# MLP up stage of a decoder trunk: four Winograd products added up in one PSUM bank with reads in between, and the P1 and P2 of three units in front

## The chip, the core and the metric

The kernel runs on one core of one Trainium2 chip. The metric is the device time of one execution in microseconds (us). The time before is 1290.3 us, the median of 3 runs (1288.57 to 1290.55). One more execution was recorded by the hardware profiler; it took 1287.94 us, and all rows of a profile below come from it.

## The reference

One layer of a decoder trunk on 1024 tokens with 1024 features: an attention sub-layer of three head groups, a gated MLP, a gated embedding, a final norm. The change is in the up half of the MLP. Cut to it:

```python
def _conv_ffn(h, w_gate, w_up, conv_w, conv_b, w_down):
    gate = h @ w_gate                       # (1024, 1024) x (1024, 2816)
    gate = causal depthwise conv of width 3 along the tokens, + conv_b
    return (jax.nn.gelu(gate) * (h @ w_up)) @ w_down
...
    h2 = _rmsnorm(r, ffn_norm[i])
    r = r + _conv_ffn(h2, w_gate[i], w_up[i], conv_w[i], conv_b[i], w_down[i])
```

All is f32. A product of two f32 matrices is made of three fp32r matmuls (`mm3`: high part of the weights by high and low part of the data, low part of the weights by the high part of the data; lines 117, 118, 119).

## The kernel before

**The units.** The 2816 columns of `w_gate` and `w_up` are taken 128 at a time: 22 units `f`. A unit makes `gs` (128 gate columns x 1024 tokens) and `us` (128 up columns x 1024 tokens), convolves `gs` into `cv`, takes its gelu, multiplies `us` by it and sends `us` to device memory (`h3_dram[f]`, line 987), from where the next stage, down, reads it.

**Seven products.** Gate and up rows, the two halves of the 1024 features and the two halves of the tokens (left, right: 512 each) make a 2 x 2 x 2 block product, and it is done with seven products in Winograd's form instead of eight. `prod(n)` is product Pn: 4 slices of 128 features by 3 matmuls, 12 matmuls of 128 x 512. With `g0` and `g1` the left and right half of `gs`, `u0` and `u1` those of `us`:

```
g0 = P1 + P2
g1 = P1 + P6 + P5 + P3
u1 = P1 + P6 + P5 + P7
u0 = P1 + P6 + P7 + P4
```

`B[n][k]` are the data operands: 1 and 2 are halves of the normalised data, 5, 3, 6, 7, 4 are made of sums and differences (`minus`, then `form`, which splits into high and low with one ScalarE cast and one VectorE subtraction, `hl`, lines 772 and 773). They are made once, after the norm `rs2`. `A[n]` are the weight operands: 1 and 2 are the halves of the gate weights (`weights_up_1`, tiles `whi`, `wlo`, two buffers each, printed `whig` and `wlog`), the rest come of sums of gate and up weights (`weights_up_2`, tiles `s13`, `s24`, `f13`, `f24`, `f4`). The loads `wg` (gate) and `wu` (up) are issued on SP's queue; `wg` lands in the one buffer `wraw`, `wu` in one of four buffers `ws`.

**PSUM before.** Bank `a` (`pg`, 3 buffers) takes P1, which ScalarE copies to `s1`, and then P2 is added to it there: `g0`. Bank `d` (`b1`, 5 buffers) takes P5 and then P3, bank `b` (`b1`) P6, P7 and P4. `s1` is added to what is read of banks `b` and `d` by VectorE: in `plus(g1, "b", s1)`, in `after5`, and in `plus(u0, "b", s1)`.

**Order.** The program is written unit after unit; a scheduler of the language places each instruction on its engine's queue by priority and by its own estimate of readiness, and it ran ahead: matmuls of unit f+1 and f+2 stand among those of f. Each engine then runs its queue strictly in order. `tc.high_priority(offset=n)` moves what is in it earlier. `gs`, `us` and `cv` have one buffer each, so that unit f+1's `gs` is written after unit f's convolution has read its own.

**The start.** Units 0 and 1 run P1 and P2 first (`early`), since `B[1]` and `B[2]` are ready before the other five operands are formed; then follow the rests. For unit 1, `s1` lies in another tile (`s1x`).

Of the kernel before, what the change touches and what calls it, by code (L numbers as in the profile page):

```python
# [17 lines left out]
F32 = mybir.dt.float32  # L18
# [4 lines left out]
ALU = mybir.AluOpType  # L23
# [52 lines left out]
def trunk(ctx: ExitStack, tc: tile.TileContext, a, out, dbg):  # L76
# [830 lines left out]
    class Unit:  # L907


        def __init__(self, f, A, s1=None):  # L910
            self.f, self.A = f, A
            self.bank = {"a": pg(f"ga{f}")}
            self.s1 = fp.tile([P, H2], F32, tag="s1", bufs=1, name=f"s1{f}") if s1 is None else s1

        def prod(self, n, to, first=False):
            if to not in self.bank:
                self.bank[to] = b1(f"g{to}{self.f}")
            wh, wl = [x.rearrange("p (k c) -> p k c", k=4) for x in self.A[n]]
            for k in range(4):
                xh, xl = B[n][k]  # L920
                mm3(self.bank[to], wh[:, k, :], wl[:, k, :], xh, xl, first and k == 0, k == 3, not first)

        def early(self):

            self.prod(1, "a", True)
            S.copy(self.s1, self.bank["a"])
            self.prod(2, "a")

        def rest(self):
            f, bank, s1 = self.f, self.bank, self.s1  # L930
# [7 lines left out]
            def plus(out, to, x):  # L938
                V.tensor_tensor(out=out, in0=bank[to], in1=x, op=ALU.add)  # L939

            def g0_done():
                S.copy(g0, bank["a"])

            def after5():
                S.copy(u1, bank["d"])  # L945
                V.tensor_tensor(out=u1, in0=u1, in1=s1, op=ALU.add)  # L946

            def g1_done():
                plus(g1, "d", g1)
                S.activation(cv, gs, AF.Identity, bias=col(C_CB + f), scale=w(2))  # L950
                V.scalar_tensor_tensor(out=cv[:, 1:], in0=gs[:, :T - 1], scalar=w(1), in1=cv[:, 1:],
                                       op0=ALU.mult, op1=ALU.add)
                V.scalar_tensor_tensor(out=cv[:, 2:], in0=gs[:, :T - 2], scalar=w(0), in1=cv[:, 2:],  # L953
                                       op0=ALU.mult, op1=ALU.add)
                S.activation(cv, cv, AF.Gelu_apprx_tanh)  # L955

            if f == 0:
                g0_done()
                self.prod(5, "d", True)
                after5()  # L960
                self.prod(3, "d")
                self.prod(6, "b", True)
                plus(g1, "b", s1)
                g1_done()
                self.prod(7, "b")
                plus(u1, "b", u1)
            else:
                if f == 1:
                    g0_done()
# [3 lines left out]
                self.prod(6, "b", True)  # L973
                plus(g1, "b", s1)
                self.prod(5, "d", True)
                after5()
                if f > 1:
                    self.prod(2, "a")
                    g0_done()
                self.prod(7, "b")  # L980
                plus(u1, "b", u1)
                self.prod(3, "d")
                g1_done()
            self.prod(4, "b")
            plus(u0, "b", s1)
            V.tensor_tensor(out=us, in0=us, in1=cv, op=ALU.mult)  # L986
            G.dma_start(h3_dram[f], us)  # L987

    lft = [t[:, half(0)] for t in r]
# [7 lines left out]
        form(5, j, lft[j], "big")  # L997
    with tc.high_priority(offset=3000):
        raw, A1 = weights_up_1(1)
    for j in range(4):  # L1000
        norm(j + 4, 1, rs2)
        form(3, j, rgt[j + 4], "big")
# [7 lines left out]
        minus(lft[j + 4], lft[j + 4], lft[j])  # L1010
        form(4, j, lft[j + 4], "r")

    s1x = cp.tile([P, T], F32, tag="rs", bufs=1, name="s1x")
# [290 lines left out]
```

## Time and profile before

| | |
|---|---|
| runs | 1290.55, 1288.57, 1290.3 us |
| profiled execution | 1287.94 us, span of its instructions 1286.2 us |
| mean granted TensorE clock | 0.994 |
| TensorE (PE) | busy 1261.6 us, 98% of the span |
| VectorE (DVE), ScalarE (ACT), GpSimd (POOL) | busy 840.8, 536.8, 103.6 us |
| MLP up stage | from 508.06 us (first matmul into `ga`) to 934.73 us (first matmul of down) |

A row of the timeline has the start in us from the start of the span, the duration in us, engine, source line, operation, output<-inputs, shape, count, and in brackets the idle time of the engine before it with what ended it. Matmuls are pipelined: one of them takes 0.39 us from start to modelled end, but the next starts long before that, so the distance of starts is what counts. A row of a window has its bounds and length, and for each engine the busy time and, behind an x, the instructions that started in it, then the granted clock of PE, the share of the DMA engines and GB/s.

### The profile page before, as it was taken

The numbers are of one execution on the slowest core, as the hardware profiler recorded it, in microseconds if no ns is written. First come the engines' busy times: TensorE is split into PE (matmuls) and PEld (weight loads), VectorE is DVE, ScalarE is ACT, GpSimd is POOL, SyncE is SP. The second block draws the span as 40 slices with busy tenths as digits, with TensorE's granted clock in tenths as the row PEclk, the third lists the DMA queues.
The fourth block names the chain that finished last, engine by engine and source line by source line (L and its number), as shares of the span: only waits on it lengthen the run. The fifth ranks groups of instructions, "written<-read, shape, count | busy, mean of one in ns | idle before, by whom it ended". The sixth has DMA issues, their size and how long they took to land.

```text
span 1286.2 us, 16285 instructions
## 1 busy us (share of the span) xinstructions
PE 1261.6 (98%) x6330; PEld 1059.1 (82%) x6330; DVE 840.8 (65%) x1410; ACT 536.8 (42%) x842; POOL 103.6 (8%) x113
## 2 busy tenths in 40 slices
PE   9999999999999999999999999999999999999996
PEld 7888888887888887788788888888888888888896
DVE  7986967567776478967776676677456123346576
ACT  6324143257675256544444334334235123334432
POOL 2000000013111231000000000000000021001010
PEclk9999999999999999999999999999999999999998
DMA  7110110111004735232222122223457216323132
GB/s 250 50 34 17 34 33 19 48 33 34 18 17 153 281 131 188 66 98 82 82 83 98 67 81 98 76 88 96 160 165 251 75 54 202 105 90 115 42 107 82
DMA packets 42237, 122.30 MB, mean 95 GB/s; under 512 B 5168, under 2 KB 7728, under 8 KB 42160
## 3 DMA queue, kind: packets, MB, share of 16 engines
q1 hardware_dynamic: 32032, 89.14, 21.4%
q0 software_dynamic: 8544, 30.41, 6.4%
q10 hardware_dynamic: 1584, 1.71, 0.4%
q8 instruction: 49, 0.80, 0.3%
q14 instruction: 28, 0.23, 0.1%
HBM read 97.13 MB, written 24.12 MB: 94 GB/s over the span
## 4 chain that ended last, share of the span: by engine, by line
PE 68%; issue 11%; POOL 2%; DVE 2%; ACT 1%; DMA 0%; DVEq 0%; POOLq 0%; ACTq 0%
PE d L119 6%; PE d L118 6%; PE d L117 6%; PE gb L119 3%; PE gb L117 3%; PE gb L118 3%; PE gd L117 2%; PE pg L117 2%; PE gd L119 2%; PE pg L119 2%; PE pg L118 2%; PE gd L118 2%; PE ga L119 2%; PE ga L118 2%; PE ga L117 2%
## 5 line engine op out<-in xcount | busy, mean ns | idle before, releaser
L119 PE MATMUL ga<-b,wlog 128*128 128x512 f32 x176 | 68.6, 390 | 0.5 <-DVE wlog L773 0.5
L117 PE MATMUL ga<-b,whig 128*128 128x512 f32 x176 | 68.9, 392 | 0.1
L117 PE MATMUL gb<-b,f 128*128 128x512 f32 x176 | 68.8, 391 | 0.0
L118 PE MATMUL gb<-b,f 128*128 128x512 f32 x176 | 68.7, 391 | 0.0
L118 PE MATMUL ga<-b,whig 128*128 128x512 f32 x176 | 68.6, 390 | 0.0
L119 PE MATMUL gb<-b,f 128*128 128x512 f32 x176 | 68.6, 390 | 0.0
L117 PE MATMUL pg<-hp,hpg 128*128 128x256 f32 (+1 forms) x192 | 61.7, 321 | 0.0
L773 DVE TENSOR_TENSOR l<-h3r,h 128x1024 fp32r<-128x1024 f32 x32 | 38.9, 1224 | 33.8 <-ACT h L772 33.6
L119 PE MATMUL pg<-hp,lpg 128*128 128x256 f32 (+1 forms) x192 | 61.0, 318 | 0.0
L118 PE MATMUL pg<-lp,hpg 128*128 128x256 f32 (+1 forms) x192 | 61.0, 318 | 0.0
L772 ACT CAST h<-h3r 128x1024 fp32r<-128x1024 f32 x34 | 35.5, 1051 | 39.9 <-PE d L118 19.2
L955 ACT ACTIVATE cv<-cv 128x1024 f32<-128x1024 f32 x22 | 23.4, 1062 | 68.2 <-DVE cv L953 68.2
L946 DVE TENSOR_TENSOR us<-us,s 128x512 f32<-128x512 f32 x21 | 14.5, 691 | 52.0 <-ACT us L945 52.0
L987 POOL DMA_DIRECT2D h3d<-us x22 | 11.7, 534 | 418.3 <-DVE us L986 418.3
L781 POOL TENSOR_TENSOR acc<-acc,sq 128x512 f32<-128x512 f32 (+1 forms) x15 | 29.1, 1938 | 166.1 <-ACT sq L780 165.8
L117 PEld LDWEIGHTS ga<-b,whig 128*128 128x128 f32 x176 | 33.0, 188 | 8.6 <-ACT s L972 1.4
L945 ACT COPY us<-gd 128x512 f32<-128x512 f32 x22 | 12.9, 588 | 64.9 <-DMA h3d<-us 59.8
L119 PEld LDWEIGHTS ga<-b,wlog 128*128 128x128 f32 x176 | 33.0, 188 | 7.9 <-DVE wlog L773 1.0
L117 PEld LDWEIGHTS gb<-b,f 128*128 128x128 f32 x176 | 33.3, 189 | 7.1 <-DVE gs L939 0.2
L119 PEld LDWEIGHTS gb<-b,f 128*128 128x128 f32 x176 | 33.2, 188 | 6.9
L118 PEld LDWEIGHTS gb<-b,f 128*128 128x128 f32 x176 | 33.2, 189 | 6.9
L118 PEld LDWEIGHTS pg<-lp,hpg 128*128 128x128 f32 x192 | 36.6, 191 | 2.6 <-DVE lp L1081 0.2
(778 smaller groups left out, 3864.2 us busy)
## 6 DMA issues: line engine op xcount, KB each, us to landing
wu<-w_gu SPq DMA_DIRECT2D x22, 512.0 KB, 3.6
wg<-w_gu SPq DMA_DIRECT2D x22, 512.0 KB, 3.5
h3d<-us POOLq DMA_DIRECT2D x22, 512.0 KB, 2.9
h3r<-h3d SPq DMA_DIRECT2D x22, 512.0 KB, 3.6
wr_wo<-w_out SPq DMA_DIRECT2D x16, 512.0 KB, 3.7
h3r<-h3d POOLq DMA_DIRECT2D x12, 512.0 KB, 3.9
x<-xT SPq DMA_DIRECT2D x16, 256.0 KB, 5.5
r<-xT SPq DMA_DIRECT2D x16, 256.0 KB, 6.8
```

What stands on the lines that cost most here:

```text
L117: TE.matmul(o, wh, xh, start=first, stop=False, skip_group_check=on)
L118: TE.matmul(o, wh, xl, start=False, stop=False, skip_group_check=on)
L119: TE.matmul(o, wl, xh, start=False, stop=last, skip_group_check=on)
L772: S.copy(hi, src)
L773: e.tensor_tensor(out=lo, in0=src, in1=hi.bitcast(F32), op=ALU.subtract)
L781: e.tensor_tensor(out=acc[:, cols], in0=acc[:, cols], in1=sq[:, cols], op=ALU.add)
L945: S.copy(u1, bank["d"])
L946: V.tensor_tensor(out=u1, in0=u1, in1=s1, op=ALU.add)
L955: S.activation(cv, cv, AF.Gelu_apprx_tanh)
L987: G.dma_start(h3_dram[f], us)
```

## The change

Product P1 goes into bank `b` as the first of a group, and P6, P7 and P4 are added to it there, in this order. The bank is read in between: after P1 (ScalarE copies it to `g0`), after P6 (ScalarE copies P1 + P6 to `g1`), after P7 (VectorE adds it to `u1`) and after P4 (VectorE multiplies it by the gelu's left half, straight into `u0`). P2 has bank `a` alone and VectorE adds it to `g0`; P5 and P3 share bank `d` as before. `s1` and `s1x` are gone. The last product of 1024 columns becomes two of 512, one of them reading the bank.

At the start P1 and P2 of units 0, 1 and 2 run before the rest. The gate weights of unit 2 are therefore loaded early, into a buffer of `ws` instead of `wraw`, and the second half of its weight work stands after unit 1's rest with a raised priority.

```diff
     def weights_up_1(f):
-        g = f4("wraw", f"wg{f}")
+        g = f4("ws" if f == 2 else "wraw", f"wg{f}")
...
-        def prod(self, n, to, first=False):
-            if to not in self.bank:
-                self.bank[to] = b1(f"g{to}{self.f}")
+        def prod(self, n):
+            to = {2: "a", 5: "d", 3: "d"}.get(n, "b")
+            first = to not in self.bank
+            if first:
+                self.bank[to] = (pg if to == "a" else b1)(f"g{to}{self.f}")
...
         def early(self):
-            self.prod(1, "a", True)
-            S.copy(self.s1, self.bank["a"])
-            self.prod(2, "a")
+            self.prod(1)
+            self.prod(2)
...
-            def g0_done():
-                S.copy(g0, bank["a"])
-            def after5():
-                S.copy(u1, bank["d"])
-                V.tensor_tensor(out=u1, in0=u1, in1=s1, op=ALU.add)
+            def copy(out, to):
+                S.copy(out, bank[to])
+            def plus(out, to):
+                V.tensor_tensor(out=out, in0=bank[to], in1=out, op=ALU.add)
...
             else:
-                if f == 1:
-                    g0_done()
-                else:
-                    self.prod(1, "a", True)
-                    S.copy(s1, bank["a"])
-                self.prod(6, "b", True)
-                plus(g1, "b", s1)
-                self.prod(5, "d", True)
-                after5()
-                if f > 1:
-                    self.prod(2, "a")
-                    g0_done()
-                self.prod(7, "b")
-                plus(u1, "b", u1)
-                self.prod(3, "d")
-                g1_done()
-            self.prod(4, "b")
-            plus(u0, "b", s1)
-            V.tensor_tensor(out=us, in0=us, in1=cv, op=ALU.mult)
+                if f > 2:
+                    self.prod(1)
+                    copy(g0, "b")
+                    self.prod(5)
+                    copy(u1, "d")
+                self.prod(6)
+                copy(g1, "b")
+                if f > 2:
+                    self.prod(2)
+                    plus(g0, "a")
+                else:
+                    self.prod(5)
+                    copy(u1, "d")
+                self.prod(7)
+                plus(u1, "b")
+                self.prod(3)
+                plus(g1, "d")
+                conv()
+            self.prod(4)
+            V.tensor_tensor(out=u0, in0=bank["b"], in1=cv[:, half(0)], op=ALU.mult)
+            V.tensor_tensor(out=u1, in0=u1, in1=cv[:, half(1)], op=ALU.mult)
             G.dma_start(h3_dram[f], us)
...
     with tc.high_priority(offset=3000):
         raw, A1 = weights_up_1(1)
+        raw2, A2 = weights_up_1(2)
...
-    units = [Unit(0, A0), Unit(1, A1, s1x[:, half(0)])]
+    units = [Unit(0, A0), Unit(1, A1), Unit(2, A2)]
     for x in units:
         x.early()
     weights_up_2(1, raw, A1)
-    for x in units:
-        x.rest()
-    for f in range(2, NF):
+    units[0].rest()
+    units[1].rest()
+    with tc.high_priority(offset=150):
+        weights_up_2(2, raw2, A2)
+    units[2].rest()
+    for f in range(3, NF):
```

In the rows of the instruction order below, a name's first number is the unit and the one after the underscore a buffer number: `gb7_5387` is bank `b` of unit 7. Equal rows that follow each other are merged (`x2`). What the program's semaphores tie together is read from the same build.

**At units 6 and 7, ScalarE's queue.** `cv` is unit 6's convolution (first row) and gelu, `whig9` the cast of unit 9's gate weights, `gs7` and `us7` are unit 7's. Before:

```order
L950 ACTIVATE cv6_5272<-gs6_5271,small_68 128x1024
L772 CAST f47_5395<-wu7_5380 128x512
L955 ACTIVATE cv6_5272<-cv6_5272 128x1024
L972 COPY s17_5399<-ga7_5398 128x512
L945 COPY us7_5402<-gd7_5430 128x512
L772 CAST whig9_5634<-wg9_5632 128x1024
L942 COPY gs7_5400<-ga7_5398 128x512
```

Now:

```order
L945 ACTIVATE cv6_5258<-gs6_5257,small_68 128x1024
L772 CAST f47_5381<-wu7_5366 128x512
L772 CAST whig9_5616<-wg9_5614 128x1024
L950 ACTIVATE cv6_5258<-cv6_5258 128x1024
L939 COPY gs7_5384<-gb7_5387 128x512 x2
L939 COPY us7_5386<-gd7_5401 128x512
```

The cast of `whig9` moved ahead of unit 6's gelu; the copy of P1 of unit 7 (first of the two copies of `gb7`) stands right behind that gelu, and P6 of unit 7 on TensorE waits for it.

**The same place, VectorE's queue**, between the sum that ends `gs6` and the second step of unit 6's convolution. Before:

```order
L939 TENSOR_TENSOR gs6_5271<-gd6_5301,gs6_5271 128x512
L773 TENSOR_TENSOR lf248_5521<-s248_5514,hf248_5520 128x1024
L951 SCALAR_TENSOR_TENSOR cv6_5272<-gs6_5271,small_68,cv6_5272 128x1023
L895 TENSOR_TENSOR s139_5640<-wu9_5638 128x512
L773 TENSOR_TENSOR f47_5395<-wu7_5380,f47_5395 128x512
L874 TENSOR_TENSOR s139_5640<-wg9_5632,wu9_5638 128x512
L874 TENSOR_TENSOR s249_5643<-s139_5640,wg9_5632 128x512
L953 SCALAR_TENSOR_TENSOR cv6_5272<-gs6_5271,small_68,cv6_5272 128x1022
```

Now:

```order
L942 TENSOR_TENSOR gs6_5257<-gd6_5274,gs6_5257 128x512
L773 TENSOR_TENSOR lf248_5505<-s248_5498,hf248_5504 128x1024
L946 SCALAR_TENSOR_TENSOR cv6_5258<-gs6_5257,small_68,cv6_5258 128x1023
L895 TENSOR_TENSOR s139_5622<-wu9_5620 128x512
L773 TENSOR_TENSOR f47_5381<-wu7_5366,f47_5381 128x512
L874 TENSOR_TENSOR s139_5622<-wg9_5614,wu9_5620 128x512
L773 TENSOR_TENSOR wlog9_5617<-wg9_5614,whig9_5616 128x1024
L874 TENSOR_TENSOR s249_5625<-s139_5622,wg9_5614 128x512
L948 SCALAR_TENSOR_TENSOR cv6_5258<-gs6_5257,small_68,cv6_5258 128x1022
```

The subtraction `wlog9` of 128 x 1024 moved between the two steps of the convolution; for units 5, 8, 11, 14 and 17 one more of the small ones (second `s24`) stands ahead of the second step too.

**At the start of the stage, VectorE's queue** after unit 0's P6. Before:

```order
L939 TENSOR_TENSOR gs0_4573<-gb0_4604,s10_4503 128x512
L895 TENSOR_TENSOR s132_4737<-wu2_4735 128x512
L773 TENSOR_TENSOR lf241_4567<-s241_4560,hf241_4566 128x1024
L874 TENSOR_TENSOR s132_4737<-wg2_4729,wu2_4735 128x512
L874 TENSOR_TENSOR s242_4740<-s132_4737,wg2_4729 128x512
L773 TENSOR_TENSOR wlog2_4732<-wg2_4729,whig2_4731 128x1024
```

Now:

```order
L942 TENSOR_TENSOR gs0_4603<-gb0_4507,gs0_4603 128x512
L874 TENSOR_TENSOR s241_4590<-wg1_4431,s241_4590 128x512
L946 SCALAR_TENSOR_TENSOR cv0_4604<-gs0_4603,small_68,cv0_4604 128x1023
L773 TENSOR_TENSOR lf241_4597<-s241_4590,hf241_4596 128x1024
L948 SCALAR_TENSOR_TENSOR cv0_4604<-gs0_4603,small_68,cv0_4604 128x1022
L895 TENSOR_TENSOR s132_4759<-wu2_4757 128x512
L773 TENSOR_TENSOR wlog3_4855<-wg3_4852,whig3_4854 128x1024
```

The last reader of unit 1's gate weights (`s241`, whose end frees `wraw` for the load of `wg3`) now stands behind the sum that reads P6 of unit 0.

On TensorE the rows are too many to show: between the end of P6 and the start of P7 of a unit, which use the same bank, stood P5 and P2 before (24 matmuls of other banks); now there stand 4 matmuls of other banks (most often of the next unit's P2). Between the last matmul of P3 of unit f and the first of P6 of unit f+1 there are 43 matmuls now, and 46 for f = 5, 8, 11, 14 and 17.

More of the change, by code (lines that the diff above doesn't have):

```diff
@@ L907, in trunk, with __init__ @@
     class Unit:
-        def __init__(self, f, A, s1=None):
+        def __init__(self, f, A):
             self.f, self.A = f, A
-            self.bank = {"a": pg(f"ga{f}")}
-            self.s1 = fp.tile([P, H2], F32, tag="s1", bufs=1, name=f"s1{f}") if s1 is None else s1
-        def prod(self, n, to, first=False):
-            if to not in self.bank:
-                self.bank[to] = b1(f"g{to}{self.f}")
+            self.bank = {}
+        def prod(self, n):
[3 more added lines that the diff above has]
+                self.bank[to] = (pg if to == "a" else b1)(f"g{to}{self.f}")
             wh, wl = [x.rearrange("p (k c) -> p k c", k=4) for x in self.A[n]]
@@ L923, in early @@
         def early(self):
-            self.prod(1, "a", True)
-            S.copy(self.s1, self.bank["a"])
-            self.prod(2, "a")
+            self.prod(1)
+            self.prod(2)
         def rest(self):
-            f, bank, s1 = self.f, self.bank, self.s1
+            f, bank = self.f, self.bank
             gs, cv, us = [f4(t, f"{t}{f}") for t in ("gs", "cv", "us")]
@@ L936, in w, with conv @@
                 return col(C_CW + 3 * f + j)
-            def plus(out, to, x):
-                V.tensor_tensor(out=out, in0=bank[to], in1=x, op=ALU.add)
-            def g0_done():
-                S.copy(g0, bank["a"])
-            def after5():
-                S.copy(u1, bank["d"])
-                V.tensor_tensor(out=u1, in0=u1, in1=s1, op=ALU.add)
-            def g1_done():
-                plus(g1, "d", g1)
+            def copy(out, to):
+                S.copy(out, bank[to])
+            def plus(out, to):
+                V.tensor_tensor(out=out, in0=bank[to], in1=out, op=ALU.add)
+            def conv():
                 S.activation(cv, gs, AF.Identity, bias=col(C_CB + f), scale=w(2))
```

22 lines of the change are left out of this document (12 added, 10 removed).

## The prediction, on record before the run

> **What bounds the kernel now.** I read the page first, then the waits of TensorE, then windows of the MLP up stage, then its timeline.
>
> ```profile
> PE 1261.6 (98%) x6330; PEld 1059.1 (82%) x6330; DVE 840.8 (65%) x1410; ACT 536.8 (42%) x842; POOL 103.6 (8%) x113
> ```
>
> TensorE is the bound: 98% busy. Time comes only out of gaps between matmuls, or goes into new ones. The windows say where gaps are in this stage:
>
> ```profile
> 508.00:545.00 37.00, 33.65 (x140) 0.95 0.28 96
> 545.00:580.00 35.00, 35.00 (x156) 1.00 0.28 90
> 580.00:640.00 60.00, 59.17 (x257) 1.00 0.24 79
> 640.00:935.00 295.00, 295.00 (x1303) 1.00 0.28 94
> ```
>
> The last row is the yardstick: 295.00 / 1303 = 0.2264 us from one matmul to the next, without a gap. By it the 140 matmuls of the first row need 31.7 us; they took 37.0: **5.3 us lost at the start of the stage**. The third row loses 60.0 - 257 x 0.2264 = 1.8, the rest nothing. So nearly all that this stage can give back is 5.3 us, and from 640 us on (1303 / 84 = 15.5 units) there are no gaps: there it can only get worse. The waits of TensorE name the gaps (us in total, times, longest):
>
> ```profile
> PE gb L117 <- ACT hf L772: 2.8, 1, 2.8
> PE ga L119 <- DVE wlog L773: 0.5, 1, 0.5
> PE gd L117 <- ACT us L945: 0.7, 1, 0.7
> ```
>
> Windows of all engines at the first of them, and VectorE's timeline there:
>
> ```profile
> 520.00:530.00 10.00, 8.36 (x37) 6.47 (x35) 10.00 (x18) 5.25 (x8) 0.00 (x0) 1.00 0.08 13
> 530.00:540.00 10.00, 8.81 (x33) 7.18 (x34) 9.04 (x12) 4.64 (x5) 0.00 (x0) 0.83 0.41 138
> ```
>
> ```profile
> 526.97 0.69 DVE L895 TENSOR_TENSOR s<-wu 128x512 f32<-128x512 f32 x1
> ```
>
> VectorE (third busy time of the windows) is full there: it forms the operands 6, 7 and 4 until 526.97, and only then begins on unit 1's sums and `f24`, for which P6 of unit 1 waits 2.8 us; after that the granted clock is 0.83.
>
> **The front, part by part.** Two more products (P1, P2 of unit 2: 24 matmuls, 5.4 us) now run before anything that needs VectorE's late work. Counting along the new order at 0.2264 us from 508.06, P7 of unit 0 comes at 508.06 + 114 x 0.2264 = 533.9, and what it needs is there: VectorE's forms end at 526.97 + 1.2 = 528.2, with `wlog` of unit 2 among them, and `f13` of unit 1 is ready near 531.8. `whig` of unit 2 waits for the end of P2 of unit 0 (two buffers) at 513.5 and is in time for 518.9. The load of its gate weights, now ahead of two others on SP's queue, delays unit 1's `wu` by one load of 3.6 to 4 us; that is read after 527. All these cost nothing, under that cover. So the old 5.3 go.
>
> A new wait comes behind them (timeline of unit 1 and 2's weight work):
>
> ```profile
> 529.37 0.69 DVE L874 TENSOR_TENSOR s<-wg,s 128x512 f32<-128x512 f32 x1
> ...
> 534.22 1.05 ACT L772 CAST whig<-wg 128x1024 fp32r<-128x1024 f32 x1 [3.08 <-DMA wg<-w_gu]
> 535.43 1.22 DVE L773 TENSOR_TENSOR wlog<-wg,whig 128x1024 fp32r<-128x1024 f32 x1
> ```
>
> From the end of the last reader (530.06) to the cast that the load frees are 4.16 us. In the new order that reader stands behind the sum which reads P6 of unit 0; P6 ends near 532.7, the reader at 534.0, the cast runs 538.2 to 539.2, `wlog` to 540.5. TensorE reaches the first P2 of unit 3 after 132 matmuls, at 537.95, and its third matmul, the first that needs `wlog`, at 538.4: 2.1 lost. VectorE is late behind it, and by the same way of counting P6 of unit 2 waits some 0.95 and P6 of unit 3 0.25 (a gap of 38 matmuls, but no `wlog` in the chain below). With 0.1 for each restart: 3.6. The front gives 5.3 - 3.6 = **1.7**.
>
> **The steady units.** This is the term that decides. P1 of unit f+1 lies in bank `b` until ScalarE has copied it to `gs`, and `gs` has one buffer: the copy stands behind the gelu of unit f. Before, P1 went to `s1`, and P6 to a bank of its own: P6 waited for no copy. Now P6 of f+1 waits for that copy, and on TensorE P7, P3, P4 and the next units' products queue behind it. Rows of the timeline: a copy between two products of one bank, then a gelu with a copy right behind it, then the links of the chain in a later unit:
>
> ```profile
> 516.96 0.39 PE L119 MATMUL ga<-b,wlog 128*128 128x512 f32 x1
> ...
> 517.39 0.59 ACT L926 COPY s1x<-ga 128x512 f32<-128x512 f32 x1
> ...
> 518.10 0.43 PE L117 MATMUL ga<-b,whig 128*128 128x512 f32 x1
> ...
> 564.89 1.06 ACT L955 ACTIVATE cv<-cv 128x1024 f32<-128x1024 f32 x1 [1.23 <-DVE cv L953]
> 565.86 0.57 ACT L942 COPY gs<-ga 128x512 f32<-128x512 f32 x1
> ...
> 722.34 0.39 PE L119 MATMUL gd<-b,lf 128*128 128x512 f32 x1
> ...
> 722.77 0.69 DVE L939 TENSOR_TENSOR gs<-gd,gs 128x512 f32<-128x512 f32 x1 [0.41 <-PE gd L119]
> ...
> 724.84 1.28 DVE L951 SCALAR_TENSOR_TENSOR cv<-gs,small,cv 128x1023 f32<-128x1023 f32 x1
> 726.04 0.68 DVE L895 TENSOR_TENSOR s<-wu 128x512 f32<-128x512 f32 x1
> ...
> 728.44 1.28 DVE L953 SCALAR_TENSOR_TENSOR cv<-gs,small,cv 128x1022 f32<-128x1022 f32 x1
> ...
> 729.82 1.06 ACT L955 ACTIVATE cv<-cv 128x1024 f32<-128x1024 f32 x1 [3.70 <-DVE cv L953]
> ```
>
> The row at 722.34 is the last matmul of P3; count from its start. First convolution step at 724.84 - 722.34 = 2.50; the four small VectorE operations between the steps take 728.44 - 726.04 = 2.40 (0.6 each), so the second step was at 6.10. Now `wlog` lies between them, 1.2: 7.30 (its cast is done at 5.1, since P2's end lets it start at 4.1). The gelu follows 1.38 after the second step's start: 8.68; the copy 565.86 - 564.89 = 0.97 after the gelu's start: 9.65; it takes 0.59: 10.24; P6 starts about 0.06 later (next fence): **10.30**. TensorE is there after 43 matmuls, so at 44 x 0.2264 = **9.96**: it waits 0.34. Where one more small operation stands ahead (units 5, 8, 11, 14, 17) it is 10.90 against 47 x 0.2264 = 10.64: 0.26. From unit 3 to unit 18 these are 11 x 0.34 + 5 x 0.26 = 5.0. Each wait has a restart. The chain of waits and TensorE's timeline at 626 us, where P3 of a unit waited for a copy, and the window around:
>
> ```profile
> 620.56 4.81 DMA h3d<-us
> ...
> 625.45 0.59 ACT us L945
> ...
> 626.09 0.50 PE gd L117
> ```
>
> ```profile
> 626.09 0.50 PE L117 MATMUL gd<-b,hf 128*128 128x512 f32 x1 [0.74 <-ACT us L945]
> 626.42 0.39 PE L118 MATMUL gd<-b,hf 128*128 128x512 f32 x1
> ```
>
> ```profile
> 620.00:640.00 20.00, 19.26 (x85) 15.55 (x84) 14.51 (x18) 7.61 (x9) 1.07 (x2) 1.00 0.24 79
> ```
>
> 0.05 from the copy's end (626.04) to the matmul, and the next one 0.33 later instead of 0.23: 0.1 each, 16 x 0.1 = 1.6.
>
> The second read in between, P6 to P7, is priced by the rows at 516.96: last matmul, copy, next matmul on that bank 1.14 us later, exactly 5 x 0.2264, with four matmuls between, as the new order has. The 0.43 instead of 0.39 says that the start was a little late: 0.05, in 18 units 0.9. [...] The row says that four matmuls of another bank are just enough, and the row decides.
>
> Units 20 and 21 have 28 matmuls in the gap and neither `wlog` nor sums in the chain (the second step at 3.7): 0.3 and 0.1, with restarts 0.6. The steady term is 5.0 + 1.6 + 0.9 + 0.6 = **8.1 lost**.
>
> **What costs or gives nothing.** VectorE saves a product of 1024 columns per unit for one of 512, and one of the additions of `s1`, about 1.2 us; it lies beside matmuls. Bank `b` is held until the gelu is done, but its buffer comes round only three units later. P3 waits for the copy of P5 into `us`, behind the transfer of the previous `us`; the timeline has the product that ends `us` and that copy:
>
> ```profile
> 711.99 1.23 DVE L986 TENSOR_TENSOR us<-us,cv 128x1024 f32<-128x1024 f32 x1
> ...
> 716.55 0.59 ACT L945 COPY us<-gd 128x512 f32<-128x512 f32 x1 [3.98 <-DMA h3d<-us]
> ```
>
> 3.3 from the end of the one to the start of the other. Now the gelu is done at 9.7, the two products at 11.3, so the copy runs from 14.6 to 15.2, and P3 comes at 10.4 + 28 x 0.2264 = 16.7. The long transfer that made the wait at 626 (4.81) eats that margin too, so I leave its cost where it is.
>
> **Sum.** -5.3 + 3.6 + 8.1 = +6.4; I take +6, since margins of 0.3 err towards less. The sum is made against the profiled execution, 1287.94 us, which lies 2.4 under the runs' median of 1290.3. Against the mean of all four executions, 1289.3: **1295.3 us**. The bounds of the unknown: waits at P6 between 0 (the chain 0.34 shorter) and 0.34 + 0.5 (a `wu` load late, which now lies in the chain), 16 x 0.5 = 8 at most and not in all units; the restart between 0 and 0.15.
>
> **Rivals.** (1) *Faster*: the copy is in time. If the chain from P3 to the copy's end is 0.34 shorter than counted (the subtraction beside another operation, an earlier cast), no P6 waits; below that point it decides. Then the steady term is 0.9, P6 of units 2 and 3 lose 1.4 less, and with a load of 3.6 instead of 4.16 the sum is -5.3 + 1.6 + 0.9 = -2.8: 1286.5. For it speaks that 0.34 is 3% of the chain; against it that the links repeat. VectorE's waits from 640 to 900 us:
>
> ```profile
> DVE gs L939 <- PE gd L119: 5.7, 14, 0.4
> DVE lf L773 <- ACT hf L772: 2.3, 14, 0.2
> DVE s L895 <- DMA wu<-w_gu: 0.3, 1, 0.3
> ```
>
> In all 14 units there the chain begins with the same waits for P3 and for its cast, and once a load was late. (2) *Same*: waits of half that size, steady 4, front as above, +1 to +2: 1291. (3) *Throttle*: after the 2.8 us gap the clock was 0.83 for ten us. If 18 short waits each brought such a stretch, 1.7 lost each, it would be +30, 1320. Against it the window 620.00:640.00: a gap of 0.74 left the clock at 1.00. [...]
>
> **How the numbers follow.** Forecast (waits at P6 outweigh the front) 0.63, at 1295.3, own range 1292 to 1300; rival 1 0.13; rival 2 0.20; rival 3 0.04. A measurement of this kernel can tell about 0.2%, 2.6 us, from no change. Slower by more: 0.63 + 0.04 = 0.67; same 0.20; faster 0.13. The range 1288.0 to 1301.0 leaves out rival 1 and rival 3, and covers the bounds.
>
> **What would show it.** Right: among TensorE's waits a new one, P6 (`gb`, line 117) for ScalarE's copy into `gs`, about 18 times and 0.1 to 0.4 us each, since the profile counts idle time only after a matmul's modelled end; windows of 60 us from 640 on with 2% fewer matmuls than 0.2264 us each would give; the wait of 2.8 at 531 gone and one of `ga` for `whig` and `wlog` near 538. Wrong: if windows from 640 on are gapless, or if PEclk drops below 1.00 there.

## The result, and the profile after

The changed kernel takes 1296.53 us (median of 6 runs, 1295.17 to 1297.41) against 1290.07 (6 runs, 1288.57 to 1290.55) for the kernel before: a ratio of 1.0051, 95% interval 1.0038 to 1.0064. It is 6.5 us slower; 1295.3 was forecast. Its profiled execution has a span of 1293.5 us, 7.3 more than that of before. The page shows why a share of busy time tells nothing here: TensorE is 98% busy as before, and VectorE has 27.5 us less to do, for no gain.

```profile
PE 1268.7 (98%) x6330; PEld 1056.6 (82%) x6330; DVE 813.3 (63%) x1388; ACT 537.2 (42%) x842; POOL 103.7 (8%) x113
```

TensorE's windows of the changed kernel, cut as in the prediction (duration, busy time, matmuls, granted clock):

```profile
508.00:545.00 37.00, 35.08 (x146) 0.96 0.18 70
545.00:580.00 35.00, 34.64 (x152) 1.00 0.30 105
580.00:640.00 60.00, 59.82 (x261) 1.00 0.24 79
640.00:935.00 295.00, 294.18 (x1273) 1.00 0.27 93
```

The first window holds 6 matmuls more than before, the last 30 fewer: 30 x 0.2264 = 6.8 us are lost where nothing was lost before. TensorE counts as 99.7% busy in that window all the same, because a matmul's busy time reaches to its modelled end; short waits are seen in the count of matmuls, or in their starts, not in the busy share.

All 1848 matmuls of the stage (22 units x 84) are in these two traces, and in those of the table further down, so the loss can be counted exactly: the time from each matmul's start to the next, less 0.2264, summed over the stage, in us.

| kernel | to 545 | 545 to 640 | 640 to 935 | from 935 | sum |
|---|---|---|---|---|---|
| before | 5.6 | 2.3 | 0.3 | 0.0 | 8.2 |
| after | 4.0 | 2.5 | 6.6 | 1.9 | 15.0 |

The difference, 6.8, is the result (0.4 more of the 7.3 had come up before the stage began). Four places make it. With them go three short waits, 0.9 together, that the kernel before had at 585, 602 and 620 us. They were of the kind that the change spreads to every unit: P2 waited, in bank `a`, for ScalarE's copy of P1 out of it.

**The front.** Timeline of the changed kernel at the first matmuls of P2 of unit 3, and the granted clock just behind it:

```profile
538.99 1.04 ACT L772 CAST whig<-wg 128x1024 fp32r<-128x1024 f32 x1 [2.48 <-DMA wg<-w_gu]
540.07 1.23 DVE L773 TENSOR_TENSOR wlog<-wg,whig 128x1024 fp32r<-128x1024 f32 x1 [0.25 <-ACT whig L772]
540.09 0.50 PE L117 MATMUL ga<-b,whig 128*128 128x512 f32 x1 [1.39 <-ACT whig L772]
541.35 0.50 PE L119 MATMUL ga<-b,wlog 128*128 128x512 f32 x1 [0.53 <-DVE wlog L773]
```

```profile
541.75:545.10 3.35, 3.35 (x10) 0.50 0.01 2
```

The old wait of 2.8 us for `hf` is gone, and in its place TensorE waits for the high and then for the low half of unit 3's gate weights: the starts are 1.55 and 0.70 us late. Then TensorE runs at half clock for 3.4 us, which costs 1.6. That is 4.0 against the 5.6 that stood there before.

**P6 of every unit from 2 on.** One unit in three views of the changed kernel: VectorE, ScalarE and TensorE from the end of P3 to P7.

```profile
655.06 1.28 DVE L946 SCALAR_TENSOR_TENSOR cv<-gs,small,cv 128x1023 f32<-128x1023 f32 x1
...
658.06 1.22 DVE L773 TENSOR_TENSOR wlog<-wg,whig 128x1024 fp32r<-128x1024 f32 x1
...
659.80 1.28 DVE L948 SCALAR_TENSOR_TENSOR cv<-gs,small,cv 128x1022 f32<-128x1022 f32 x1
```

```profile
661.17 1.06 ACT L950 ACTIVATE cv<-cv 128x1024 f32<-128x1024 f32 x1 [3.50 <-DVE cv L948]
662.14 0.57 ACT L939 COPY gs<-gb 128x512 f32<-128x512 f32 x1
```

```profile
652.57 0.39 PE L119 MATMUL gd<-b,lf 128*128 128x512 f32 x1
...
662.31 0.39 PE L118 MATMUL ga<-b,whig 128*128 128x512 f32 x1
662.76 0.50 PE L117 MATMUL gb<-b,hf 128*128 128x512 f32 x1
663.09 0.39 PE L118 MATMUL gb<-b,hf 128*128 128x512 f32 x1
...
666.29 0.39 PE L119 MATMUL ga<-b,wlog 128*128 128x512 f32 x1
666.52 0.44 PE L117 MATMUL gb<-b,f 128*128 128x512 f32 x1
666.79 0.40 PE L118 MATMUL gb<-b,f 128*128 128x512 f32 x1
```

The copy of P1 (662.14) stands behind the gelu (661.17), that behind the second convolution step (659.80), and `wlog` lies ahead of that. The first matmul of P6 starts 0.06 after the copy's end, and 0.45 after the matmul before it instead of 0.23: 0.22 late. The next comes after 0.33: 0.11 for the restart. The first of P7 is on time, the second 0.05 late. This repeats from unit to unit, 0.22 where 43 matmuls lie between P3 and P6, 0.14 where 46 do, about 0.4 in all each time.

**Behind P3 of unit 21.** VectorE and TensorE of the changed kernel near the end of the stage:

```profile
927.80 0.68 DVE L986 TENSOR_TENSOR us<-us,cv 128x512 f32<-128x512 f32 x1
```

```profile
936.40 0.50 PE L117 MATMUL gd<-b,hf 128*128 128x512 f32 x1 [1.60 <-ACT us L939]
```

The product that ends `us` of unit 20 is done at 928.5, and the copy into the next `us` comes only at 935.8, behind the transfer: P3 starts 1.76 late, and its second matmul 0.11. From 928 to 936 us the DMA engines moved 284 GB/s (91 from 900 to 910); that this traffic made the transfer long was not tested.

**The wait near 626**, for the same kind of copy (0.90 and 0.11 by the starts), is gone.

### The profile page after: what moved, and what is told of

Read it like the earlier page. It is cut to its first block, busy times and chain, and to the rows that moved or that the text cites. A ratio compares the mean times of both kernels' runs of the same rounds, so it can differ in the third digit from the quotient of the medians.

```text
span 1293.5 us, 16213 instructions
## 1 busy us (share of the span) xinstructions
PE 1268.7 (98%) x6330; PEld 1056.6 (82%) x6330; DVE 813.3 (63%) x1388; ACT 537.2 (42%) x842; POOL 103.7 (8%) x113
## 4 chain that ended last, share of the span: by engine, by line
PE 44%; issue 34%; POOL 2%; DVE 2%; ACT 1%; DMA 1%; DVEq 0%; POOLq 0%; ACTq 0%
PE d L117 6%; PE d L119 6%; PE d L118 6%; PE pg L117 2%; PE pg L118 2%; PE pg L119 2%; PE o L117 2%; PE o L119 2%; PE o L118 2%; PE z_bq L119 1%; POOL h3d L987 1%; PE z_bq L117 1%; PE z_bq L118 1%; PE pob L633 1%; PE pob L632 1%
## 5 line engine op out<-in xcount | busy, mean ns | idle before, releaser
L942 DVE TENSOR_TENSOR us<-gb,us 128x512 f32<-128x512 f32 x22 | 15.2, 691 | 101.2 <-PE gb L119 98.3
L939 ACT COPY gs<-gb 128x512 f32<-128x512 f32 x43 | 24.9, 578 | 64.4 <-PE gb L119 64.4
L987 POOL DMA_DIRECT2D h3d<-us x22 | 11.8, 535 | 425.1 <-DVE us L986 389.4
L772 ACT CAST f<-s 128x1024 fp32r<-128x1024 f32 x22 | 23.2, 1054 | 37.4 <-PE gb L119 32.7
L119 PEld LDWEIGHTS pg<-hp,lpg 128*128 128x128 f32 x192 | 36.6, 190 | 2.5
L117 PEld LDWEIGHTS pg<-hp,hpg 128*128 128x128 f32 x192 | 36.6, 190 | 2.5
L117 PE MATMUL gb<-b,hf 128*128 128x512 f32 x88 | 36.6, 416 | 1.2 <-ACT gs L939 0.4
L117 PE MATMUL ga<-b,whig 128*128 128x512 f32 x88 | 34.8, 395 | 1.4 <-ACT whig L772 1.4
```

The costliest lines, as they stand in the source:

```text
L117: TE.matmul(o, wh, xh, start=first, stop=False, skip_group_check=on)
L119: TE.matmul(o, wl, xh, start=False, stop=last, skip_group_check=on)
L772: S.copy(hi, src)
L939: S.copy(out, bank[to])
L942: V.tensor_tensor(out=out, in0=bank[to], in1=out, op=ALU.add)
```

## The experiments

My theory, A: the steady loss is the wait of P6 for the copy into the one buffer `gs`. Its rivals: B, a read of a bank between two products that add up in it costs TensorE by itself; C, the front makes the loss. All runs were timed in five rounds, with the kernel before beside them on the same chip (three chips in all). The times, each with the median of before on its chip, and the loss by place:

| kernel | us (before) | ratio, 95% | to 545 | 545 to 640 | 640 to 935 | from 935 | sum |
|---|---|---|---|---|---|---|---|
| bank only | 1296.70 (1289.52) | 1.0067 (1.0053 to 1.0081) | 5.5 | 2.1 | 6.7 | 1.5 | 15.8 |
| front only | 1289.69 (1289.52) | 1.0009 (1.0000 to 1.0018) | 2.6 | 6.1 | 2.3 | 0.0 | 11.0 |
| own tile | 1284.74 (1289.52) | 0.997 (0.996 to 0.998) | 0.9 | 3.0 | 0.3 | 0.0 | 4.2 |
| longer chain | 1296.38 (1289.52) | 1.0056 (1.0043 to 1.007) | 3.9 | 2.0 | 7.4 | 1.6 | 14.8 |
| longer chain, VectorE | 1298.55 (1289.95) | 1.0063 (1.0051 to 1.0076) | 3.5 | 3.4 | 8.2 | 0.7 | 15.9 |
| copy before gelu | 1289.40 (1289.95) | 1.000 (0.9991 to 1.0009) | 4.0 | 3.2 | 1.4 | 0.0 | 8.6 |
| bank, own tile | 1288.25 (1289.95) | 0.9982 (0.9973 to 0.9991) | 5.1 | 1.5 | 0.3 | 0.0 | 6.9 |
| own tile, halves | 1285.38 (1289.95) | 0.9965 (0.9952 to 0.9977) | 1.1 | 4.3 | 0.3 | 0.0 | 5.6 |
| own tile at the front | 1293.35 (1289.43) | 1.003 (1.0019 to 1.0042) | 1.0 | 2.0 | 8.6 | 0.0 | 11.7 |
| convolution first | 1289.03 (1289.43) | 0.9994 (0.9985 to 1.0003) | 3.6 | 3.9 | 0.3 | 0.0 | 7.8 |
| own tile, conv. first | 1284.67 (1289.43) | 0.9962 (0.9949 to 0.9975) | 0.9 | 3.0 | 0.3 | 0.0 | 4.2 |

In "longer chain, VectorE" 16 matmuls of down stand among those of the last unit; they are counted as steps like the others.

### P1 copied to a tile of its own

```diff
+            s1 = fp.tile([P, H2], F32, tag="s1", bufs=1, name=f"s1{f}")
...
-                    copy(g0, "b")
+                    copy(s1, "b")
...
-                    plus(g0, "a")
+                    V.tensor_tensor(out=g0, in0=bank["a"], in1=s1, op=ALU.add)
```

> The new order with one thing undone: ScalarE's copy of P1 goes to a half tile of its own, as before the change, and the addition of P2 writes it into gs. The copy no longer stands behind the gelu of the unit before. The scheduler then also puts P2 as a whole between P6 and P7. Theory A (P6 waits for that copy, because gs has one buffer): the 0.14 to 0.22 us at P6 with its restart of 0.11 and the 0.05 at P7 go in all units from 3 on, 18 x 0.4 = 7 us; 1288 to 1291 us, and 60-us windows from 640 on with 264 to 265 matmuls. Rival B (a read of a bank between two products that add up in it costs TensorE its 0.38 us per unit, wherever the copy goes): the bank is still read twice in between, 1295 to 1297. Rival C (the front makes the loss): 1295 to 1297, windows from 640 on gapless.

Measured: 1284.74 us, 0.3% faster than before the change and 3 us better than theory A expected. TensorE's windows of this kernel, and its ScalarE and TensorE at one unit:

```profile
508.00:545.00 37.00, 36.76 (x161) 1.00 0.20 72
...
640.00:935.00 295.00, 295.00 (x1303) 1.00 0.29 96
```

```profile
800.84 0.59 ACT L940 COPY s<-gb 128x512 f32<-128x512 f32 x1 [2.10 <-PE gb L119]
802.55 1.06 ACT L951 ACTIVATE cv<-cv 128x1024 f32<-128x1024 f32 x1 [1.12 <-DVE cv L949]
```

```profile
803.14 0.39 PE L119 MATMUL gd<-b,f 128*128 128x512 f32 x1
803.37 0.39 PE L117 MATMUL gb<-b,hf 128*128 128x512 f32 x1
```

The copy now comes 0.4 us after P1 and ahead of the gelu, P6 0.23 after the matmul before it, and the stretch from 640 on is gapless with 1303 matmuls. The bank is still read twice between products: rival B falls. What the theory had not expected is the front: it is nearly gapless too (0.9 lost), at full clock. The load of unit 3's gate weights is no earlier there (the cast starts at 539.42, against 538.99). But in this kernel P6 of unit 1 is free of the gelu of unit 0, and the scheduler, which works out when each input is ready, issues its 12 matmuls, 2.7 us, ahead of P2 of unit 3, which begins 144 matmuls into the stage instead of 132:

```profile
539.42 1.05 ACT L772 CAST whig<-wg 128x1024 fp32r<-128x1024 f32 x1 [2.90 <-DMA wg<-w_gu]
...
541.41 0.39 PE L117 MATMUL ga<-b,whig 128*128 128x512 f32 x1
...
541.87 0.43 PE L119 MATMUL ga<-b,wlog 128*128 128x512 f32 x1
```

So both losses of the change may hang on the one buffer `gs`. That is a hypothesis here; it is tested further down.

### The bank alone, the front alone

The first kernel has the shared bank and the reads in between, with units 0 and 1 in front as before the change; the second has the banks and `s1` of before, with the first three units in front.

```diff
-    units = [Unit(0, A0), Unit(1, A1), Unit(2, A2)]
+    units = [Unit(0, A0), Unit(1, A1)]
...
-    for f in range(3, NF):
+    for f in range(2, NF):
```

> The first half of the change alone: the shared bank, read in between, with only units 0 and 1 in front as before. Theory A: the steady loss is there in full (units 2 to 20, 19 x 0.4 = 7.5, and up to 1.9 at P3 of unit 21), and of the old front's 5.3 us some is still lost: 1296 to 1300. Rival C (the front of three units makes the loss): 1288 to 1291.

```diff
-    units = [Unit(0, A0), Unit(1, A1, s1x[:, half(0)])]
+    units = [Unit(0, A0), Unit(1, A1, s1x[:, half(0)]), Unit(2, A2, s1x[:, half(1)])]
...
-                if f > 1:
+                if f > 2:
                     self.prod(2, "a")
```

> The second half alone: P1 and P2 of the first three units in front, each unit with its own banks and s1 as before the change. Theory A: no steady loss, the old 5.3 us at the front traded for the wait for unit 3's weights and the slow clock behind it (3.5 to 5): 1288 to 1291. Rival C: 1295 to 1297.

The bank alone costs 7.2 us, as much as the whole change; the front alone 0.2. Rival C falls. TensorE's windows of the bank alone:

```profile
508.00:545.00 37.00, 34.00 (x141) 0.95 0.30 99
...
640.00:935.00 295.00, 294.25 (x1274) 1.00 0.27 92
```

The front of three units by itself only moves its waits. TensorE's longest waits in this stage there (us in total, times, longest):

```profile
PE gb L117 <- DVE gs L939: 2.3, 2, 1.2
...
PE gd L117 <- ACT us L945: 1.7, 2, 0.9
...
PE ga L117 <- ACT s L972: 1.4, 1, 1.4
...
PE gb L117 <- ACT hf L772: 0.9, 1, 0.9
```

Its profiled execution (1292.22 us, 2.5 above its median) lost 2.8 more than that of before (11.0 against 8.2) where the medians differ by 0.2, with an interval that ends at 0.18%, 2.3 us: the one profile of each does not settle it closer.

### A longer chain: two attempts at a dose

```diff
+                S.activation(cv, cv, AF.Identity)
                 S.activation(cv, cv, AF.Gelu_apprx_tanh)
```

> The changed kernel with one more ScalarE pass over cv (it multiplies nothing, 1.06 us busy) ahead of each gelu; TensorE's order of products in the steady units stays as it is but for one matmul. Theory A: the copy of P1, and with it P6, comes 0.97 us later in every unit from 3 to 20, since that is a loop with no slack: 18 x 0.97 = 17 us, 1311 to 1316. Rival B and rival C (nothing waits for the gelu): 1296 to 1298.

```diff
+                V.tensor_tensor(out=gs[:, half(0)], in0=gs[:, half(0)], in1=gs[:, half(0)], op=ALU.max)
                 V.scalar_tensor_tensor(out=cv[:, 2:], in0=gs[:, :T - 2], scalar=w(0), in1=cv[:, 2:],
```

> The changed kernel with one more VectorE operation on gs (512 columns, maximum of gs with itself, which changes nothing) ahead of the second convolution step: 0.60 us more in the chain that ends with the copy of P1, which stays behind the gelu. TensorE has 43 matmuls between P3 and P6 in every unit, as in most of the changed kernel, and one to four between P6 and P7. Theory A2: the wait at P6 grows from 0.14 to 0.22 by 0.6 in 18 units: 11 us, 1305 to 1310, in the trace 0.8 at each P6. Rival B and rival C (nothing in that chain holds TensorE): 1295 to 1298, P6 as in the changed kernel.

(A2 is theory A with a correction that the first of these two runs gave, below.) Both expectations failed: 1296.38 us where 1311 to 1316 was expected, and 1298.55 (ratio 1.0063, 1.0051 to 1.0076) where 1305 to 1310 was. Taken by the times alone they would speak for B or C. The traces say that neither edit lengthened the chain by what it added: P6 of most units from 3 on waits 0.14 to 0.27 in the first kernel and 0.27 to 0.38 in the second, against 0.14 to 0.26 in the changed one. ScalarE of the first:

```profile
660.85 1.06 ACT L950 ACTIVATE cv<-cv 128x1024 f32<-128x1024 f32 x1 [3.85 <-DVE cv L948]
661.81 0.57 ACT L939 COPY gs<-gb 128x512 f32<-128x512 f32 x1
662.28 1.06 ACT L951 ACTIVATE cv<-cv 128x1024 f32<-128x1024 f32 x1
```

The copy went between the added pass and the gelu. It does not need the gelu at all: it only has to wait until the last reader of `gs`, the second convolution step, is done, and in the changed kernel the gelu merely stood ahead of it on ScalarE. VectorE of the second:

```profile
680.46 1.28 DVE L946 SCALAR_TENSOR_TENSOR cv<-gs,small,cv 128x1023 f32<-128x1023 f32 x1
...
684.08 0.68 DVE L948 TENSOR_TENSOR gs<-gs 128x512 f32<-128x512 f32 x1
684.68 0.68 DVE L874 TENSOR_TENSOR s<-wg,s 128x512 f32<-128x512 f32 x1
685.28 1.27 DVE L949 SCALAR_TENSOR_TENSOR cv<-gs,small,cv 128x1022 f32<-128x1022 f32 x1
```

The scheduler moved `wlog` (1.2 us) out from between the two steps; the added operation and one more small one (0.6 each) took its place. From the last matmul of P3 (677.97) to the first of P6 (688.23) are 10.26 us, against 10.19 in the changed kernel. So by their times these two runs don't tell the theories apart; they correct theory A in one point (the copy waits for the second step, and for the gelu only by its place in ScalarE's order) and suggest the next run. No edit gave a clean dose. One came by itself, in the first of the two kernels, the last matmul of P3 and the first of P6 of one unit:

```profile
671.48 0.39 PE L119 MATMUL gd<-b,lf 128*128 128x512 f32 x1
...
682.05 0.50 PE L117 MATMUL gb<-b,hf 128*128 128x512 f32 x1 [0.44 <-ACT gs L939]
```

VectorE stood idle for 0.30 us between the convolution steps of that unit (what held it is not shown), its second step came 0.39 later behind P3 than in the changed kernel, and the way from P3 to P6 is 10.57 us instead of 10.19 with the same 43 matmuls in between. P6 waits 0.60 by the starts instead of 0.22: the 0.38 that the chain grew arrived at P6 whole, as theory A says and B does not.

### The chain made shorter, in two ways

```diff
-                    copy(g0, "b")
+                    with tc.high_priority(offset=1000):
+                        copy(g0, "b")
```

> The changed kernel, gs with its one buffer, but ScalarE's copy of P1 has priority over the gelu: it then waits only for the second convolution step, the last reader of gs, and comes 0.97 us earlier. From unit 9 on the scheduler issues the products in the order of the code, 12 matmuls between P6 and P7. TensorE's order at the front is that of the changed kernel: eight matmuls of P2 of unit 3 stand ahead of P6 of unit 1. Theory A2 (P6 waits for the second convolution step and then for the gelu that stands between it and the copy on ScalarE): the steady 7 us go, and up to 1.9 at P3 of unit 21; the front's wait for unit 3's weights and the slow clock behind it stay: 1288 to 1291 us, the first window 508 to 545 at 145 to 148 matmuls. Rival B (the read in between costs 0.38 per unit by itself): 1295 to 1297. Rival D (the one buffer costs at the front too, e1's gain there hangs on the tile of its own): the same 1288 to 1291, so D is told apart by the first window alone: gapless under no theory.

(e1 in it is the tile of its own.)

```diff
             def conv():
+                with tc.high_priority(offset=3500):
...
```

> The changed kernel with gs as it is and the convolution and the gelu given priority over all weight work, so that neither wlog nor the small additions stand between the two convolution steps. Theory A2: the chain from the last matmul of P3 to the end of the copy of P1 falls from 10.2 to about 7 us, TensorE needs 36 x 0.2264 = 8.2 for P4, P1 and P5 between them: no wait at P6, the products in the order of the code, and the front as in the changed kernel: 1288 to 1291. Rival (wlog then comes late, and P1 or P2 waits for it): 1293 to 1300, with waits of ga or gb for wlog in each unit.

1289.40 and 1289.03 us, both within theory A's 1288 to 1291, with `gs` still in one buffer and the bank still read in between. ScalarE and TensorE of the first, where the copy now stands ahead of the gelu:

```profile
806.47 0.59 ACT L939 COPY gs<-gb 128x512 f32<-128x512 f32 x1 [3.71 <-DVE cv L948]
806.95 1.06 ACT L950 ACTIVATE cv<-cv 128x1024 f32<-128x1024 f32 x1
```

```profile
807.14 0.39 PE L119 MATMUL gd<-b,f 128*128 128x512 f32 x1
807.36 0.39 PE L117 MATMUL gb<-b,hf 128*128 128x512 f32 x1
```

and TensorE's windows of the second:

```profile
508.00:545.00 37.00, 34.53 (x149) 0.99 0.24 82
...
640.00:935.00 295.00, 295.00 (x1303) 1.00 0.28 94
```

The steady loss is gone in the second and all but gone in the first (1.4 us are left from 640 to 935, the last of them at 675, before the order of the code is reached), and the late wait of unit 21 with it, while the front's stays (4.0 and 3.6 us in the first window). Three different edits (a tile of its own, another place in ScalarE's queue, a shorter chain on VectorE) each remove the steady loss: its cause is the chain that ends with that copy.

None of the three edits changes one thing alone. In each the scheduler also put the products in the order of the code, with 36 matmuls between P3 and P6 instead of 43 or 46. That is 8.4 us of cover instead of 10.0 or 10.6, so the order by itself would have made the wait longer. And with the copy ahead of the gelu `wlog` left its place between the convolution steps too: the chain from P3 to the copy's end is 8.1 us there (798.98 to 807.06), 2.1 less than the 10.14 of the changed kernel, of which the gelu is 0.97. With the convolution first it is 7.2.

### The tile of its own at the front alone, and without the third unit

```diff
+            if f < 3:
+                s1 = fp.tile([P, H2], F32, tag="s1", bufs=1, name=f"s1{f}")
...
             if f < 3:
-                copy(g0, "b")
-                plus(g0, "a")
+                copy(s1, "b")
+                V.tensor_tensor(out=g0, in0=bank["a"], in1=s1, op=ALU.add)
```

> The changed kernel with a half tile of its own for the copy of P1 in units 0 to 2 alone; from unit 3 on the copy goes to gs as in the changed kernel, and from unit 5 on TensorE's order is that of the changed kernel, with the same 43 and 46 matmuls between P3 and P6. At the front P6 of unit 1 no longer waits for the gelu of unit 0 and stands, with four matmuls of P5, ahead of P2 of unit 3: 16 matmuls, 3.6 us of cover for unit 3's weights. Theory (two separate losses, both from the one buffer gs): the front's 4.1 us (1.55 + 0.70 + 0.22 of restarts + 1.6 of half clock) and the 0.5 at P6 of unit 2 go, the steady 0.4 per unit and the 1.9 at unit 21 stay: 1291 to 1293; windows from 640 on with 260 to 261 matmuls in 60 us. Rival (the front's wait is set by the load of unit 3's weights and comes back somewhere else behind it): 1295 to 1297. The gains of the two halves should add up: 1296.5 - 1289.4 = 7.1 (copy ahead of the gelu, front unchanged) plus this one should give 1296.5 - 1284.7 = 11.8, so 4.7 here, 1291.8.

1293.35 us: slightly above the 1291 to 1293 expected, well below the rival's 1295 to 1297. TensorE's windows:

```profile
508.00:545.00 37.00, 36.76 (x161) 1.00 0.23 82
...
640.00:935.00 295.00, 292.70 (x1266) 1.00 0.28 94
```

The front is as gapless as with the tile of its own in all units (TensorE's order there is the same, so the cover ahead of P2 of unit 3 is 12 matmuls more than in the changed kernel and not 16: P5 of unit 1 stands ahead of it in both). The steady loss is whole (with the late wait of 1.75, which now falls inside this window, 8.6). By the loss in the profiles the two halves nearly add up: 15.0 - 8.6 = 6.4 for the copy ahead of the gelu, 15.0 - 11.7 = 3.3 for this one, 9.7 together against 15.0 - 4.2 = 10.8 for the tile of its own. (By the medians it is 7.1 and 3.2 against 11.8. The 4.7 expected of this kernel counted the front's whole loss as gained, and 1.0 of it stays.) So the front's loss hangs on the same buffer: the order that the copy forces on TensorE leaves P2 of unit 3 without cover.

The kernel with the bank and the tile of its own, but two units in front:

> The shared bank with P1 copied to a half tile of its own, and only units 0 and 1 in front. Against the tile of its own with three units in front (1284.7) it tells what the third unit in front is worth; against the bank alone (1296.7) what the tile of its own is worth. Theory: from 640 on gapless; at the front P6 or P5 of unit 1 waits again for what VectorE does after 527, some 3 to 5 us with the slow clock: 1287 to 1290. Rival E (the third unit in front brings nothing, the freed P6 alone fills the front): 1284 to 1286.

1288.25 us, as expected: gapless from 640 on, 5.1 us lost at the front. The third unit in front is worth 1288.25 - 1284.74 = 3.5 us once the copy is free (3.1 when each is taken against before on its own chip, 2.7 by the losses, 6.9 - 4.2), and rival E falls.

### Two candidates

```diff
-            G.dma_start(h3_dram[f], us)
+            for i in range(2):
+                G.dma_start(h3_dram[f][:, half(i)], us[:, half(i)])
```

> The tile of its own with three units in front, and the transfer of us to memory issued as two, one per half, so that ScalarE's copy of P5 into the right half waits for one half alone. Theory: the wait of 0.9 for that copy near 625 and its restart go, 0.7 us in all: 1283.5 to 1285. Rival: two issues on POOL's queue and twice the descriptors make the transfer later: 1284.5 to 1287.

> The tile of its own in all units together with the priority of the convolution: a candidate, to see whether anything is left behind the tile of its own. us is done sooner, its transfer begins sooner, and the wait of 0.9 near 625 for that transfer may go: 1283.5 to 1285; if the weight work now comes late, 1286 to 1290.

Neither takes anything off the tile of its own beyond the scatter. With two transfers (1285.38) the wait of P3 for the copy into `us` (1.05 at 625.6 with the tile of its own) did not go but moved to 570 us and grew:

```profile
PE gd L117 <- ACT us L940: 2.6, 2, 2.1
```

With the convolution first (1284.67) it is spread over three places. The best version is thus the change with P1 copied to a tile of its own: 0.997 of before, interval 0.996 to 0.998, and 11.8 us less than the change as made.

## Why the prediction was right, point by point

**Held.** The bound (gaps between matmuls of one engine) and the sign. The steady wait, its place, its cause and nearly its size: the chain from the last matmul of P3 to P6 was worked out as 10.30 and is 10.19, so P6 waits 0.22 and 0.14 where 0.34 and 0.26 were said; the restart 0.11 for 0.1; P7 0.05 as said. Per unit that is 0.4 instead of 0.5, and over units 4 to 21, which the steady term counts, 7.2 instead of 8.1. The gelu is in that chain by its place in ScalarE's order alone, which the prediction did not say. That VectorE's saving is worth nothing held (27.5 us less work, nothing faster). That the old wait for `hf` would go held.

**Mis-sized: the front.** The term "5.3 - 3.6 = 1.7" measured 5.6 - 4.0 = 1.6 up to 545, and behind it P6 of unit 2 lost 0.53 and P6 of unit 3 0.22, each with 0.11, 1.0 together: the front gave some 0.6. The cast came at 538.99 for a forecast 538.2, so the wait is 2.25 (1.55 + 0.70), not 2.1. The half clock behind it, 1.6 us, was in the row that the prediction quoted from before (0.83 over ten us) but not in its sum.

**Near in sum, partly by luck.** The forecast was +6 and the medians differ by 6.5, but misses of some 1 to 2 us cancel in it: the front gave 1.1 less than forecast and the wait behind P3 of unit 21 cost 1.9 that no term had, while the steady term was 0.9 too large and waits of 1.0 (near 626) and 0.9 (P2 for the copy of P1, between 580 and 620) went that the sum had left in place.

**Wrong step, hidden by the sum.** "I leave its cost where it is", of the wait near 626: it went (1.0), and the same kind of wait came up at unit 21 (1.76 and 0.11). The margin of P3 over the copy of P5 was worked out for the steady units with a transfer of usual length; at the end of the stage the transfer took longer, 7.3 us from the end of the product to the copy instead of 3.3, and the late gelu had used up the margin.

**Wrong step: what would show it.** TensorE's list of waits was to show P6 about 18 times. It shows it once:

```profile
PE gb L117 <- ACT gs L939: 0.4, 1, 0.4
```

The others leave 0.1 us or less between the modelled end of one matmul and the start of P6 (0.06 in the rows above: 662.31 + 0.39 against 662.76), and the list has none so short. The answer for the tile, which has TensorE's weight loads too, shows them (us, times; 20 of the 41 stand before P6, 21 before P7); so do the starts, and the count of matmuls per window that the prediction also named.

```profile
  PEld gb L117: 13.6, 41
```

**The rivals.** The copy in time (faster): refuted in the changed kernel by every unit from 2 on. Yet it was near: P6 waits 0.22 at the end of a chain of 10.19, so by these rows a chain 2% shorter would have ended in time. No run cut it by so little; the kernels without the wait cut 2 us and more of it, or took the copy out of it. Throttle: the clock is 1.00 from 640 on, so the short waits there (0.14 to 0.26 at P6) didn't draw it. The read in between P6 and P7 cost little by itself: with four matmuls of another bank in between, the second matmul of P7 was 0.05 late in the changed kernel, and with twelve in between, in the kernel with the tile of its own, P7 was not late (808.80 to 809.03, a step of 0.23).

**Not seen in advance.** The prediction took the front's wait for a matter of the late load of unit 3's weights. The load is as late in the kernel with the tile of its own and costs nothing there: the order in which TensorE gets to P2 of unit 3 was the cause, and that order followed from the copy behind the gelu.

## What to carry to other kernels

A PSUM bank that is read between two products joined the engine that reads it to TensorE's queue here: in units 3 to 21 P6 came 0.14 to 0.26 us late, behind ScalarE's copy out of the bank. So look at where the read stands in that engine's order and what its output buffer waits for, not only at the bank. Here a half tile of 2 KB per partition turned a loss of 6.5 us into a gain of 4.8. Before timing a "dose" of work, look up in the trace whether it landed in the chain it was meant for; with a scheduler between the code and the chip, the two doses here did not. And look at what else moved: the edits here that removed the wait also changed the order of other work.

## What the runs showed of the hardware

**The slow clock.** In eight of the thirteen traces TensorE's granted clock fell in this stage. Its mean from 508 to 545 us was 0.95 in before, the bank alone, the copy before the gelu and the bank with the tile of its own, and 0.96 in the changed kernel and with the longer chain; it was 0.98 and from 545 to 580 us 0.97 with the longer chain on VectorE, and 0.99 and 0.96 with the convolution first. In before it was 0.50 from 530.68 to 534.09 us, in the changed kernel from 541.73 to 545.14, 3.41 us each time, and 1.00 ahead of it and behind it up to the end of the stage. Up to the fall, TensorE had come 2.48 us late in before, in one wait, and 2.47 in the changed kernel (1.55 and 0.70, with their restarts). With the two transfers a wait of 2.1 near 570 us left the clock at 1.00 (mean from 545 to 580), and so did the 1.87 at unit 21 of the changed kernel (1.76 and 0.11; mean from 935 to 942). What makes it fall after the one wait and not after the other was not shown.

**Near 69 us from the start** of the program the granted clock differs between the profiled executions as well: from 68 to 74 us its mean was 0.72 in the front alone and in the tile of its own at the front, and 1.00 in before and in the changed kernel. So the losses were compared within the stage, not by spans.

**A wait costs more than its length:** at full clock, the matmul behind the late one started 0.33 to 0.34 us after it instead of 0.23 in all five waits of over 0.12 us of this stage in before and in all 23 in the changed kernel.
